# Ten of 24 gate tiles as five pairs of seven block products, in a stage of their own ahead of the attention

## The chip, the cores and the metric

The kernel runs on one NeuronCore of one Trainium2 chip. The metric is device time in microseconds of one execution of the whole program; lower is better. Several runs of one kernel are told by their median.

## The reference

One layer of a decoder trunk on 1024 tokens of width 1024, in float32:

```python
u = rmsnorm(x)
pool_v, q, k, v, f, z, xbc, dt, gate_logits = split_columns(u @ w_in)
y_A, y_B, y_C = pool(pool_v) @ p_pool, attention(q, k, v, f) @ p_attn, ssd(z, xbc, dt) @ p_ssd
g = sigmoid(gate_logits)                       # three gates of width 1024
x = x + (g[0] * y_A + g[1] * y_B + g[2] * y_C) @ w_out
x = x + conv_ffn(rmsnorm(x)) @ w_down          # conv_ffn: u @ w_up, causal conv, silu gate
```

The change concerns `gate_logits`: 3072 columns of the first product, handled as 24 tiles of 128 columns each.

## The kernel before, in words

Every product is a float32 product made of three products of a faster format: each operand is split into a high and a low part (`hi` by a copy on ScalarE, `lo` by a subtraction on VectorE), and `mm3` (L117) issues hi·hi, hi·lo and lo·hi into one PSUM bank. The normalized input stands transposed in SBUF for the whole first half, as `uh` and `ul`, two halves of 512 tokens each. One output tile (128 columns by 1024 tokens) takes 8 blocks of the inner dimension x 2 halves x 3 = 48 matmuls of 512 columns. `load_w` (L107) brings its weights (512 KB, one staging buffer `wraw`) and splits them into one of three buffer pairs `whi`, `wlo`.

Gate tile i is made by `gate` (L270): the product, a copy or sigmoid on ScalarE (L280, L282), and a store to `g_d` in DRAM, from where `gate_now` (L595) fetches it when a branch is merged. Tiles below `NGATE1` (L441) get their sigmoid at once, the others in `gate_now` (L602).

The stages in order:

1. Small projections, the pool mixer, then the SSD for two groups of heads (L581 to L584). The SSD's chunks are chains of small steps over all engines.
2. Eight gates (`run(gates())`, L585), with `p_big` as PSUM tile, then the values of the attention, `in_proj_tok` (L587), token by token: 8 tiles of 24 matmuls.
3. The attention, for four pairs of heads (L762 to L771). `attend` (L733) runs eight units per pair: scores (L673, L674), softmax on VectorE and ScalarE (L675 to L685), transposes of the probabilities (L697), their split (L702, L105), and the product with V (L722). `others` (L751) makes the queries and keys of the next pair (96 matmuls) and then the 5, 5, 4 and 2 gates that `GCUT` (L442) gives to each pair.
4. The merging of three branches (L784, L815, L818), the output product, and the feed-forward part. There the up product is already made in pairs of tiles by a scheme of seven block products in place of eight (`pair`, L1050, `prod`, L1007, `split_next`, L987): 2 x 2 blocks of weights and of the normalized input are added and subtracted beforehand, and their products combined after. Nine of the pairs have two products made earlier.

Each engine runs its instructions in an order that the framework fixes when the program is built, from a timeline of its own: what stands earlier in the program goes first, and where its operands are not ready in that timeline, later work is put in its place. So in the SSD and in the attention, gate products stand between the steps of the chains. The order does not change while the kernel runs.

Of the kernel before, what the change touches and what calls it, by code (L numbers as in the profile page):

```python
# [15 lines left out]
P = 128  # L16
# [30 lines left out]
def hybrid_kernel(ctx: ExitStack, tc: tile.TileContext, x, xT, w_in, w_z, w_v, w_fd, mixw, p_pool, p_attn,  # L47
# [33 lines left out]
    def bank():  # L81
        return pst("bank")
# [21 lines left out]
    def sub_lo(eng, lo, src, hi):  # L104
        eng.tensor_tensor(lo, src, hi.bitcast(F32), op=ALU.subtract)  # L105
# [93 lines left out]
    def run(gen):  # L199
        while True:  # L200
            try:
                next(gen)
            except StopIteration as e:
                return e.value
# [62 lines left out]

    g_d = dpool.tile([24, P, 1024], F32, name="g_d")

    def gate(i, halves):  # L270

        if halves:
            parts = in_proj_halves(T_GATE + i)
        else:
            ps = in_proj(T_GATE + i)
            parts = [(slice(h * 512, (h + 1) * 512), ps[:, h * 512:(h + 1) * 512]) for h in range(2)]
        for hs, ps in parts:
            gt = gpool.tile([P, 512], F32, name="gt")
            if i < NGATE1:
                nc.scalar.activation(gt, ps, AF.Sigmoid)  # L280
            else:
                nc.scalar.copy(gt, ps)  # L282
            nc.sync.dma_start(g_d[i][:, hs], gt)
# [157 lines left out]
    NGATE1 = 8  # L441
    GCUT = (0, 5, 10, 14, 16)  # L442
    v_d = dpool.tile([NATT, P, NT, 256], F32, name="v_d")
    yn_d = dpool.tile([NT, P, 1024], F32, name="yn_d")
    with ExitStack() as st:
# [130 lines left out]
        def gates():  # L576
            for i in range(NGATE1):
                gate(i, False)
                yield

# [4 lines left out]
        run(gates())  # L585

        for t, ps in in_proj_tok([w_v[kp, 0] for kp in range(4)], sp):  # L587
            vs = sp.tile([P, 8, 2, 64], R32, name="vs", tag="xs", bufs=5)
            pv = ps.rearrange("p (h d) -> p h d", d=64)
            nc.scalar.copy(vs[:, :, 0, :], pv)  # L590
            sub_lo(nc.vector, vs[:, :, 1, :], pv, vs[:, :, 0, :])
            nc.sync.dma_start(v_d[:, :, t, :].rearrange("r p c -> p r c"),
                              vs.bitcast(F32).rearrange("p (r h) x d -> p r (h x d)", h=2))
# [250 lines left out]
    def hl(t):  # L844
        return t[:, 0], t[:, 1]

    HL = [P, 2, 4, 512]
    LO, HI = slice(0, 512), slice(512, 1024)
    B11, B21, B22 = [hl(slot(i, HL, R32, n)) for i, n in enumerate(("b11", "b21", "b22"))]

    with ExitStack() as st:
# [77 lines left out]
        def up_load(n):  # L929

            if n < FT:
                q = 2 * ((n + 1) % 2)
                for x in range(2):
                    nc.sync.dma_start(ab[:, q + x, :], f_up[2 * ORDER[n] + x])

        for j in range(5):
            w = load_w(w_out[j])
            if j == 1:
                for i in range(2):
                    nc.sync.dma_start(ab[:, i, :], f_up[2 * i])  # L940
                up_load(0)
            for h in range(2):
                run(out_tile(j, h, w))
# [12 lines left out]

# [3 lines left out]
        LATE, ALL = ("S1", "S2", "S4", "S3"), ("A11", "S1", "S2", "A12", "S4", "S3")  # L960
        ring, parts = [], {}
        todo = []
        for n in range(FT + 1):
            names = [(n, name) for name in (() if n == FT else LATE if ORDER[n] < NPRE else ALL)]
            if n > 0:
                names.insert(names.index((n, "S2")) if names else 0, (n - 1, "A22"))
            todo += names
        n_split = [0]
        s12, s34 = None, ss

        def up_block(n, name):
            if name[0] == "S":
                t, c = (s12, s34)[(int(name[1]) - 1) // 2], (LO, HI)[(int(name[1]) - 1) % 2]
                return t[:, c]
            return ab[:, 2 * ((n + 1) % 2) + int(name[1]) - 1, (LO, HI)[int(name[2]) - 1]]

        SUMS = {"S1": ("A21", "A22", ALU.add), "S2": ("S1", "A11", ALU.subtract), "S3": ("A11", "A21", ALU.subtract),
                "S4": ("A12", "S2", ALU.subtract)}

        def up_sum(n, *names):  # L980

            if n < FT:
                for name in names:
                    x, y, op = SUMS[name]
                    nc.vector.tensor_tensor(up_block(n, name), up_block(n, x), up_block(n, y), op=op)

        def split_next():  # L987

            if n_split[0] == len(todo):
                return  # L990
            n, name = todo[n_split[0]]
            hi, lo = ring[n_split[0] % len(ring)]
            n_split[0] += 1
            src = up_block(n, name)
            nc.scalar.copy(hi, src)
            sub_lo(nc.vector, lo, src, hi)
            parts[n, name] = hi, lo
            if name == "A22":
                up_load(n + 2)
            if name == "S2":  # L1000
                if n == 0:
                    up_load(1)
                up_sum(n + 1, "S1", "S2")
            if name == "S3":
                up_sum(n + 1, "S4", "S3")

        def prod(ps, n, name, b, first=True):  # L1007

            w = parts[n, name]
            for k in range(4):  # L1010
                c = slice(k * P, (k + 1) * P)
                m = mm3([ps], (w[0][:, c], w[1][:, c]), [(b[0][:, k, :], b[1][:, k, :])], first and k == 0, k == 3,
                        skip_group_check=not first)
            split_next()
            return m

        def conv_act(i, ca, cb):

            v, g = [sp.tile([P, 1024], F32, name="vg", bufs=2) for _ in range(2)]
            for t, c, acc in ((2 * i + 1, cb, v), (2 * i, ca, g)):  # L1020
                w = [vec[:, V_FW + 3 * t + k:V_FW + 3 * t + k + 1] for k in range(3)]
                nc.scalar.activation(acc, c, AF.Identity, bias=vec[:, V_FB + t:V_FB + t + 1], scale=w[2])  # L1022
                for s in (1, 2):
                    nc.vector.scalar_tensor_tensor(out=acc[:, s:], in0=c[:, 0:1024 - s], scalar=w[2 - s],  # L1024
                                                   in1=acc[:, s:], op0=ALU.mult, op1=ALU.add)
            nc.scalar.activation(g, g, AF.Silu)
            nc.vector.tensor_tensor(g, g, v, op=ALU.mult)
            nc.sync.dma_start(act_d[i], g)
# [21 lines left out]
        def pair(n, c, last):  # L1050


            i = ORDER[n]
            ca, cb = c
            chain, b5 = bank(), bank()
            if i < NPRE:
                for x, t in ((0, cb[:, LO]), (1, ca[:, LO])):
                    nc.sync.dma_start(t, pre_d[i, x])
            else:
                prod(chain, n, "A11", B11)  # L1060
                nc.scalar.copy(ca[:, LO], chain)
            prod(b5, n, "S1", T1)
            nc.scalar.copy(cb[:, HI], b5)
            if last is not None:
                fourth(n - 1, *last)
            prod(chain, n, "S2", T2, first=i < NPRE)
            if i < NPRE:
                nc.tensor.matmul(chain, lhsT=ident, rhs=cb[:, LO], start=False, stop=True, skip_group_check=True)  # L1068
            nc.scalar.copy(ca[:, HI], chain)
            if i >= NPRE:  # L1070
                b2 = bank()
                prod(b2, n, "A12", B21)
                nc.vector.tensor_tensor(ca[:, LO], ca[:, LO], b2, op=ALU.add)
            prod(b5, n, "S4", B22, first=False)
            nc.vector.tensor_tensor(ca[:, HI], ca[:, HI], b5, op=ALU.add)
            prod(chain, n, "S3", T3, first=False)
            nc.vector.tensor_tensor(cb[:, HI], cb[:, HI], chain, op=ALU.add)
            return chain, c

        def fourth(n, chain, c):  # L1080
            prod(chain, n, "A22", T4, first=False)
            nc.scalar.copy(c[1][:, LO], chain)
            conv_act(ORDER[n], *c)

# [4 lines left out]
        for i in range(NPRE + 1):  # L1089
# [14 lines left out]
            if i == 2:  # L1104
                s12 = wpool.tile([P, 1024], F32, name="wraw", bufs=WRAW)
                up_sum(0, "S1", "S2", "S4", "S3")
# [4 lines left out]
        for _ in range(3):  # L1111
            hi, lo = [wpool.tile([P, 1024], R32, name=n, bufs=WHL) for n in ("whi", "wlo")]
            ring += [(hi[:, c], lo[:, c]) for c in (LO, HI)]
        ring += [(more[:, 0, r, :], more[:, 1, r, :]) for r in range(4)]
        for _ in range(len(ring)):
            split_next()
        last = None
        for i in range(FT):
            last = pair(i, (cc[:, 2 * (i % 2)], cc[:, 2 * (i % 2) + 1]), last)
        fourth(FT - 1, *last)  # L1120


# [205 lines left out]
```

## Time and profile before

| | before |
|---|---|
| time, median of 3 runs | 1877.31 us (1876.27 to 1879.17) |
| time of the profiled execution | 1876.14 us |
| its span, first to last instruction | 1874.4 us |
| TensorE busy | 98% of the span |
| VectorE busy | 58% |
| ScalarE busy | 46% |
| mean granted TensorE clock | 0.995 of full speed |

PE is TensorE, PEld its weight loads, DVE VectorE, ACT ScalarE, POOL GpSimd, SP the engine whose queue issues most transfers. Matmuls are pipelined: the recorded duration of one (about 0.39 us) overlaps the next, so what one costs is read as the distance between starts: the length of an unbroken piece divided by its matmuls. Some matmul records can be missing from a count.

### The profile page before, as it was taken

The page shows a single profiled execution, that of the slowest core. Times are in us where ns is not written, and L with a number is a line of the kernel's source. Part 1 is how long each engine was busy: PE and PEld are TensorE (multiplying, and loading weights), DVE is VectorE, ACT ScalarE, POOL GpSimd, SP SyncE. Part 2 cuts the span into 40 slices and gives each one's busy share as a digit, 9 for nine tenths or more (in the row PEclk, how much of TensorE's full clock was granted, in tenths as well). Part 3 has the DMA queues.
Part 4 walks back from the last instruction along what each step waited for, and adds up shares of the span by engine and source line. Part 5 has one row for each costly group of instructions (what it writes and reads, how often), then busy time and mean ns, then how long its engine had stood idle before and what let it go on. Part 6 is the DMA issues. An engine that isn't in the chain of part 4 may idle for free.

```text
span 1874.4 us, 22365 instructions
## 1 busy us (share of the span) xinstructions
PE 1841.7 (98%) x8622; PEld 1504.7 (80%) x8622; DVE 1086.6 (58%) x1611; ACT 856.8 (46%) x1384; POOL 157.1 (8%) x119
## 2 busy tenths in 40 slices
PE   7999999999999999999999999999999999999997
PEld 6888888888878778787788888878888888888886
DVE  6752682661265553655765432878787887743424
ACT  5343584573255463654633322545454555533221
POOL 0100240330000000000022002320000000000000
PEclk9999999999999999999999999999999999999998
DMA  4231231333511313124364451443333321664532
GB/s 153 84 120 34 85 108 57 101 130 104 175 65 62 107 51 129 40 90 153 121 200 135 145 180 68 152 135 124 102 107 118 104 91 53 214 235 157 180 102 68
DMA packets 81629, 217.35 MB, mean 116 GB/s; under 512 B 8625, under 2 KB 15217, under 8 KB 80754
## 3 DMA queue, kind: packets, MB, share of 16 engines
q1 hardware_dynamic: 76192, 201.82, 31.9%
q0 software_dynamic: 1728, 8.39, 1.4%
q10 hardware_dynamic: 3602, 5.72, 0.9%
q8 instruction: 67, 1.10, 0.2%
q14 instruction: 40, 0.33, 0.1%
HBM read 164.41 MB, written 51.48 MB: 115 GB/s over the span
## 4 chain that ended last, share of the span: by engine, by line
PE 93%; DVE 2%; DMA 2%; ACT 1%; issue 1%; POOL 0%; SPq 0%; DVEq 0%; ACTq 0%; POOLq 0%
PE p_bank L123 40%; PE p_big L123 19%; PE p_half L123 17%; PE p_bank L265 2%; PE p_bank L264 2%; PE p_bank L263 2%; PE p_po L722 2%; PE p_sc L674 2%; PE p_pt L697 2%; PE p_bank L557 1%; PE p_sc L673 1%; PE p_bank L1068 0%; DMA yi<-yn_d 0%; PE p_bank L324 0%; DMA ab<-in_f_up_dram 0%
## 5 line engine op out<-in xcount | busy, mean ns | idle before, releaser
L105 DVE TENSOR_TENSOR wlo<-wraw,whi 128x1024 fp32r<-128x1024 f32 (+1 forms) x109 | 126.3, 1159 | 162.8 <-ACT whi L112 161.3
L123 PE MATMUL p_bank<-act,whi 128*128 128x512 f32 (+1 forms) x736 | 218.5, 381 | 0.0
L123 PE MATMUL p_big<-uh,whi 128*128 128x512 f32 (+1 forms) x416 | 157.4, 379 | 0.5 <-ACT whi L112 0.5
L123 PE MATMUL p_big<-uh,wlo 128*128 128x512 f32 (+1 forms) x416 | 157.2, 378 | 0.5 <-DVE wlo L105 0.5
L123 PEld LDWEIGHTS p_bank<-act,whi 128*128 128x128 f32 x736 | 136.0, 188 | 26.6
L123 PE MATMUL p_big<-ul,whi 128*128 128x512 f32 (+1 forms) x416 | 156.7, 377 | 0.0
L123 PE MATMUL p_half<-uh,whi 128*128 128x512 f32 x384 | 153.4, 399 | 0.0
L123 PE MATMUL p_half<-ul,whi 128*128 128x512 f32 x384 | 153.0, 399 | 0.0
L123 PE MATMUL p_half<-uh,wlo 128*128 128x512 f32 x384 | 152.2, 397 | 0.0
L112 ACT CAST whi<-wraw 128x1024 fp32r<-128x1024 f32 x81 | 84.9, 1048 | 137.6 <-PE p_big L123 68.4
L123 PE MATMUL p_bank<-act,wlo 128*128 128x512 f32 (+1 forms) x368 | 139.2, 381 | 0.0
L123 PE MATMUL p_bank<-t,whi 128*128 128x512 f32 x440 | 137.2, 391 | 0.0
L123 PE MATMUL p_bank<-b,whi 128*128 128x512 f32 x376 | 118.9, 397 | 2.2 <-ACT whi L1046 2.0
L1024 DVE SCALAR_TENSOR_TENSOR vg<-cc,vec,vg 128x1023 f32<-128x1023 f32 (+1 forms) x88 | 110.3, 1278 | 8.4 <-ACT vg L1022 8.3
L105 DVE TENSOR_TENSOR wlo<-stage,whi 128x1024 fp32r<-128x1024 f32 x44 | 54.1, 1230 | 101.2 <-ACT whi L112 101.0
L112 ACT CAST whi<-stage 128x1024 fp32r<-128x1024 f32 x44 | 46.1, 1051 | 115.2 <-PE p_bank L123 106.7
L123 PEld LDWEIGHTS p_bank<-t,whi 128*128 128x128 f32 x440 | 82.6, 188 | 17.8
L123 PE MATMUL p_bank<-t,ring 128*128 128x512 f32 x396 | 96.4, 391 | 0.0
L172 POOL TENSOR_TENSOR ss<-ss,vg 128x512 f32<-128x512 f32 (+1 forms) x21 | 30.0, 1429 | 763.7 <-ACT vg L171 763.5
L123 PEld LDWEIGHTS p_big<-uh,wlo 128*128 128x128 f32 x416 | 78.9, 190 | 14.6 <-DVE wlo L105 0.8
L123 PEld LDWEIGHTS p_big<-uh,whi 128*128 128x128 f32 x416 | 79.0, 190 | 14.2 <-ACT whi L112 0.9
L123 PEld LDWEIGHTS p_big<-ul,whi 128*128 128x128 f32 x416 | 79.0, 190 | 13.5
(307 smaller groups left out, 4067.7 us busy)
## 6 DMA issues: line engine op xcount, KB each, us to landing
ab<-in_f_up_dram SPq DMA_DIRECT2D x53, 512.0 KB, 3.3
wraw<-in_w_in_dram SPq DMA_DIRECT2D x48, 512.0 KB, 3.4
stage<-in_f_down_dram SPq DMA_DIRECT2D x44, 512.0 KB, 3.5
g_d<-gt SPq DMA_DIRECT2D x48, 256.0 KB, 2.0
gt<-g_d SPq DMA_DIRECT2D x48, 256.0 KB, 3.4
act_d<-vg SPq DMA_DIRECT2D x22, 512.0 KB, 3.0
stage<-act_d SPq DMA_DIRECT2D x22, 512.0 KB, 4.5
mt<-acs_d SPq DMA_DIRECT2D x16, 512.0 KB, 4.4
```

Of the source, the lines that this page charges most:

```text
L105: eng.tensor_tensor(lo, src, hi.bitcast(F32), op=ALU.subtract)
L112: nc.scalar.copy(hi, raw)
L123: m = nc.tensor.matmul(o, lhsT=wt, rhs=ah[part], start=first and i == 0, stop=last and i == 2, **kw)
L172: eng.tensor_tensor(ss, ss, sq, op=ALU.add)
L263: nc.tensor.matmul(ps, lhsT=a, rhs=hi[:, c], start=k == 0, stop=False)
L264: nc.tensor.matmul(ps, lhsT=a, rhs=lo[:, c], start=False, stop=False)
L265: nc.tensor.matmul(ps, lhsT=ul[t // 4][:, k, q], rhs=hi[:, c], start=False, stop=k == NT - 1)
L557: nc.tensor.matmul(py[:, d], lhsT=mt[:, h * P:(h + 1) * P], rhs=xd[:, d], start=True, stop=True)
L674: nc.tensor.matmul(pss[:, 0:w], lhsT=Q2[h][hp, qs], rhs=KL[hp, j0:j0 + w], start=False, stop=True)
L697: nc.tensor.transpose(pt[:, off + (i - qq[0]) * P:off + (i - qq[0] + 1) * P], in_=probs[i][:, kb * P:(kb + 1) * P], identity=ident)
L722: nc.tensor.matmul(po[:, q0:q0 + w], lhsT=VV[:, kb, h, :], rhs=t[:, o:o + w], start=pc == 0 and i == 0, stop=last and i == len(prods) - 1)
L1024: nc.vector.scalar_tensor_tensor(out=acc[:, s:], in0=c[:, 0:1024 - s], scalar=w[2 - s], in1=acc[:, s:], op0=ALU.mult, op1=ALU.add)
```

## The change

The scheme of seven products becomes a class used in two places. The 24 gates are now made so: tiles 0 to 5 plainly beside the SSD; tiles 6 to 15 as five pairs in a new stage between the SSD and the attention; tiles 16 to 23 in the attention, 1, 2, 2 and 3 for its four pairs of heads. A pair splits seven 512-column blocks (A11, A12, A22 and four sums S1 to S4 of weight blocks), multiplies each with one block of the input (B11, B21, B22, or T1 to T4, which are sums of input blocks made once on VectorE while the values of the attention are multiplied), and combines the results on ScalarE and VectorE. Buffers: two pairs of raw weights `ab`, the three `whi`/`wlo` pairs as a ring of six half tiles, `s12` in the place of `wraw`, eight PSUM banks. `NGATE1` is 16, so 16 sigmoids in `gate_now` fall away and those 16 are taken when the gate is made. The feed-forward part uses the same class, with the calls in the order they had.

```diff
+    class BlockProduct:
+        LATE, ALL = ("S1", "S2", "S4", "S3"), ("A11", "S1", "S2", "A12", "S4", "S3")
+        SUMS = {"S1": ("A21", "A22", ALU.add), "S2": ("S1", "A11", ALU.subtract),
+                "S3": ("A11", "A21", ALU.subtract), "S4": ("A12", "S2", ALU.subtract)}
...
+        def load(self, n):
+            if n < len(self.order):
+                for x in range(2):
+                    nc.sync.dma_start(self.ab[:, 2 * ((n + 1) % 2) + x, :], self.src(self.order[n], x))
...
+        def split_next(self):
...
+            nc.scalar.copy(hi, src)
+            sub_lo(nc.vector, lo, src, hi)
+            self.parts[n, name] = hi, lo
+            if name == "A22":
+                self.load(n + 2)
+            if name == "S2":
+                if n == 0:
+                    self.load(1)
+                self.sums(n + 1, "S1", "S2")
+            if name == "S3":
+                self.sums(n + 1, "S4", "S3")
...
+        def prod(self, ps, n, name, b, first=True):
+            w, b = self.parts[n, name], self.blocks[b]
+            for k in range(4):
+                c = slice(k * P, (k + 1) * P)
+                mm3([ps], (w[0][:, c], w[1][:, c]), [(b[0][:, k, :], b[1][:, k, :])], first and k == 0, k == 3,
+                    skip_group_check=not first)
+            self.split_next()
...
-    NGATE1 = 8
-    GCUT = (0, 5, 10, 14, 16)
+    NPLAIN, NGATE1 = 6, 16
+    GCUT = (0, 1, 3, 5, 8)
...
-        run(gates())
-
-        for t, ps in in_proj_tok([w_v[kp, 0] for kp in range(4)], sp):
...
+        for i in range(NPLAIN):
+            gate(i, False)
+    psum(bank=(512, 8))
+    with ExitStack() as st:
+        tp = pool("t", stack=st)
...
+        def t_sums(sp):
+            for k in range(4):
+                f = {}
+                for n, h, k0 in (("T1", 0, k), ("T3", 1, k), ("T2", 1, k + 4), ("T4", 0, k + 4)):
+                    f[n] = sp.tile([P, 512], F32, name=f"f{n}", bufs=1)
+                    nc.vector.tensor_tensor(f[n], uh[h][:, k0, :].bitcast(F32), ul[h][:, k0, :].bitcast(F32),
+                                            op=ALU.add)
+                for n, x, y in (("T1", "T3", "T1"), ("T3", "T2", "T3"), ("T2", "T2", "T1"), ("T4", "T4", "T2")):
+                    nc.vector.tensor_tensor(f[n], f[x], f[y], op=ALU.subtract)
+                    hi, lo = blocks[n]
+                    nc.scalar.copy(hi[:, k, :], f[n])
+                    sub_lo(nc.vector, lo[:, k, :], f[n], hi[:, k, :])
+                yield
+        def gates_done(i, ca, cb):
+            for x, c in enumerate((ca, cb)):
+                for hs in (LO, HI):
+                    gt = gpool.tile([P, 512], F32, name="gt")
+                    nc.scalar.activation(gt, c[:, hs], AF.Sigmoid)
+                    nc.sync.dma_start(g_d[2 * i + x][:, hs], gt)
...
+        gp.load(0)
+        with ExitStack() as st2:
+            sp = pool("v", bufs=2, stack=st2)
+            ts = t_sums(sp)
+            for t, ps in in_proj_tok([w_v[kp, 0] for kp in range(4)], sp):
+                vs = sp.tile([P, 8, 2, 64], R32, name="vs", bufs=1)
...
+                next(ts, None)
+        gp.s12 = wpool.tile([P, 1024], F32, name="wraw", bufs=WRAW)
+        gp.sums(0, "S1", "S2", "S4", "S3")
+        sp = pool("gp", stack=st)
+        gp.run(w_ring(), sp.tile([P, 4, 1024], F32, name="cc"))
```

## Rows read from the trace of the kernel before

**Rows 1.** The page: span, busy time by engine, chain by engine.

```profile
span 1874.4 us, 22365 instructions
...
PE 1841.7 (98%) x8622; PEld 1504.7 (80%) x8622; DVE 1086.6 (58%) x1611; ACT 856.8 (46%) x1384; POOL 157.1 (8%) x119
...
PE 93%; DVE 2%; DMA 2%; ACT 1%; issue 1%; POOL 0%; SPq 0%; DVEq 0%; ACTq 0%; POOLq 0%
```

**Rows 2.** Busy time in stretches: SSD, gates and V, three head pairs, attention's end.

```profile
core 0: us, PE busy (x) PEld busy (x) DVE busy (x) ACT busy (x) POOL busy (x), PEclk, DMA share, GB/s
339.00:421.00 82.00, 80.89 (x440) 68.59 (x438) 58.16 (x85) 56.66 (x117) 32.85 (x24) 1.00 0.37 126
421.00:501.00 80.00, 80.00 (x357) 66.29 (x356) 14.84 (x22) 19.37 (x27) 1.30 (x1) 1.00 0.33 110
522.90:634.70 111.80, 111.80 (x537) 87.83 (x537) 60.46 (x118) 59.50 (x111) 0.53 (x1) 1.00 0.22 72
634.70:749.00 114.30, 114.30 (x543) 88.78 (x541) 60.62 (x118) 58.95 (x107) 0.53 (x1) 1.00 0.27 89
749.00:849.00 100.00, 100.00 (x484) 78.14 (x483) 57.09 (x113) 54.82 (x101) 0.00 (x0) 1.00 0.19 64
885.00:910.00 25.00, 20.94 (x107) 16.03 (x106) 18.92 (x42) 17.79 (x37) 0.00 (x0) 0.93 0.49 169
```

**Rows 3.** Chain in order of time: plain gates, gates in the attention, feed-forward pairs.

```profile
421.47 36.35 PE p_big L123 x160
...
523.76 5.71 PE p_half L123 x24
...
737.55 9.29 PE p_half L123 x41
...
1534.80 77.32 PE p_bank L123 x338
```

**Rows 4.** Groups by line in the first head pair, 522.9 to 634.7 us.

```profile
L123 PE MATMUL p_half<-uh,wlo 128*128 128x512 f32 x113 | 44.6, 395 | 0.0
...
L105 DVE TENSOR_TENSOR wlo<-wraw,whi 128x1024 fp32r<-128x1024 f32 x7 | 8.6, 1224 | 9.1 <-ACT whi L112 9.1
L112 ACT CAST whi<-wraw 128x1024 fp32r<-128x1024 f32 x8 | 8.4, 1047 | 9.0 <-PE p_half L123 6.3 <-DMA wraw<-in_w_in_dram 1.4 <-issue 1.3
L282 ACT COPY gt<-p_half 128x512 f32<-128x512 f32 x9 | 5.3, 585 | 6.3 <-PE p_half L123 6.3
```

**Rows 5.** Timeline of PE and DVE at two places of the first head pair.

```profile
565.09 0.71 PE L697 MATMUL p_pt<-cst,ns 128*128 128x128 f32 x5
...
566.30 0.69 DVE L105 TENSOR_TENSOR pl<-p_pt,ph 128x512 fp32r<-128x512 f32 x1 [0.20 <-ACT ph L702]
...
571.51 0.28 PE L722 MATMUL p_po<-pl,VV 128*128 128x256 f32 x1
...
582.28 0.60 PE L697 MATMUL p_pt<-cst,ns 128*128 128x128 f32 x4
...
583.53 0.69 DVE L105 TENSOR_TENSOR pl<-p_pt,ph 128x512 fp32r<-128x512 f32 x1 [0.24 <-ACT ph L702]
...
588.64 0.28 PE L722 MATMUL p_po<-pl,VV 128*128 128x256 f32 x1
```

**Rows 6.** Groups by line, 339 to 501 us: prices of 512-column steps.

```profile
L280 ACT ACTIVATE gt<-p_big 128x512 f32<-128x512 f32 x16 | 8.7, 595 | 0.1
...
L561 DVE TENSOR_TENSOR zs<-yt,zs 128x512 f32<-128x512 f32 x8 | 5.5, 684 | 0.1
...
L551 ACT CAST sth<-state 128x512 fp32r<-128x512 f32 x7 | 4.3, 615 | 0.0
```

**Rows 7.** Waits of DVE in the feed-forward pairs: total, times, longest.

```profile
DVE wraw L985 <- DMA ab<-in_f_up_dram: 24.8, 9, 4.5
```

More of the change, by code (lines that the diff above doesn't have):

```diff
@@ L268, in hybrid_kernel, with w_ring @@
+    def w_ring():
+        ring = []
+        for _ in range(WHL):
+            hi, lo = [wpool.tile([P, 1024], R32, name=n, bufs=WHL) for n in ("whi", "wlo")]
+            ring += [(hi[:, c], lo[:, c]) for c in (LO, HI)]
+        return ring
     g_d = dpool.tile([24, P, 1024], F32, name="g_d")
@@ L275, in gate @@
             ps = in_proj(T_GATE + i)
-            parts = [(slice(h * 512, (h + 1) * 512), ps[:, h * 512:(h + 1) * 512]) for h in range(2)]
+            parts = [(hs, ps[:, hs]) for hs in (LO, HI)]
         for hs, ps in parts:
@@ L574, in ssd_chunks @@
                 yield
[L576 to L579, printed above, removed]
         a0 = run(ssd_inputs(0))
@@ L584, in hybrid_kernel @@
         run(ssd_chunks(1, *a1))
-        run(gates())
-        for t, ps in in_proj_tok([w_v[kp, 0] for kp in range(4)], sp):
[L588 to L593, printed above, removed]
+        for i in range(NPLAIN):
+            gate(i, False)
@@ L842, in hybrid_kernel @@
     pre_d = dpool.tile([NPRE, 2, P, 512], F32, name="pre_d")
[L844 to L848, printed above, removed]
     B11, B21, B22 = [hl(slot(i, HL, R32, n)) for i, n in enumerate(("b11", "b21", "b22"))]
@@ L927, in hybrid_kernel, with conv_act, early_results @@
         ab = slot(3, [P, 4, 1024], F32, "ab")
[L929 to L934, printed above, removed]
+        def conv_act(i, ca, cb):
+            v, g = [sp.tile([P, 1024], F32, name="vg", bufs=2) for _ in range(2)]
+            for t, c, acc in ((2 * i + 1, cb, v), (2 * i, ca, g)):
+                w = [vec[:, V_FW + 3 * t + k:V_FW + 3 * t + k + 1] for k in range(3)]
+                nc.scalar.activation(acc, c, AF.Identity, bias=vec[:, V_FB + t:V_FB + t + 1], scale=w[2])
+                for s in (1, 2):
+                    nc.vector.scalar_tensor_tensor(out=acc[:, s:], in0=c[:, 0:1024 - s], scalar=w[2 - s],
+                                                   in1=acc[:, s:], op0=ALU.mult, op1=ALU.add)
+            nc.scalar.activation(g, g, AF.Silu)
+            nc.vector.tensor_tensor(g, g, v, op=ALU.mult)
+            nc.sync.dma_start(act_d[i], g)
+        def early_results(i, p1, c11):
+            for x, t in ((0, p1), (1, c11)):
+                nc.sync.dma_start(t, pre_d[i, x])
+        up_blocks = {"B11": B11, "B21": B21, "B22": B22}
+        up = BlockProduct(ORDER, lambda i, x: f_up[2 * i + x], up_blocks, ab, conv_act, NPRE, early_results)
+        up.s34 = ss
         for j in range(5):
@@ L940, in hybrid_kernel @@
                     nc.sync.dma_start(ab[:, i, :], f_up[2 * i])
-                up_load(0)
+                up.load(0)
             for h in range(2):
@@ L958, in hybrid_kernel @@
         T3, T4 = [hl(slot(4 + i, HL, R32, f"t{3 + i}")) for i in range(2)]
[L960 to L1028, printed above, removed]
+        up_blocks.update(T1=T1, T2=T2, T3=T3, T4=T4)
@@ L1048, in early_w @@
             return hi, lo
[L1050 to L1083, printed above, removed]
         ew = [early_w(i) for i in range(2)]
@@ L1104, in hybrid_kernel @@
             if i == 2:
-                s12 = wpool.tile([P, 1024], F32, name="wraw", bufs=WRAW)
-                up_sum(0, "S1", "S2", "S4", "S3")
+                up.s12 = wpool.tile([P, 1024], F32, name="wraw", bufs=WRAW)
+                up.sums(0, "S1", "S2", "S4", "S3")
         for _ in n:
@@ L1110, in hybrid_kernel @@
         cc = upool.tile([P, 4, 1024], F32, name="cc", tag="ul1")
[L1111 to L1120, printed above, removed]
+        up.run(w_ring() + [(more[:, 0, r, :], more[:, 1, r, :]) for r in range(4)], cc)
         stage = slot(3, [P, 4, 1024], F32, "stage")
```

79 lines of the change are left out of this document (added).

## The prediction

> **What bounds the kernel now.** I read the page first. TensorE is busy for 98% of the span, VectorE for 58%, ScalarE for 46%, and 93% of the chain that ended last is TensorE [rows 1]. A busy share can hide waits, because recorded durations overlap, so I went on to the stretches that the change touches. In each of them TensorE has work almost all the time: the second half of the SSD, the stretch with the remaining gates and V, and the attention, at a granted clock of 1.00, which is the 2.4 GHz level. Only at the end of the attention do 4.1 us in 25 stand idle, at a clock of 0.93 [rows 2]. The third view is the chain in order of time, for the distance between matmuls: 36.35 us for 160 plain gate matmuls, that is 0.2272 us each; 77.32 us for 338 in the feed-forward pairs, 0.2288 us; in the attention 0.2266 us (41 in a piece) to 0.2379 us (24 in a piece, the start of a piece after other work costs about 0.1 us more) [rows 3]. So every stretch is a queue of matmuls, and a matmul that goes is worth its distance, as long as those that stay still cover the waits of the SSD's and the attention's chains. That condition is the question of this change.
>
> **What goes and comes on TensorE.** Plain gates: two fewer before the attention, 2 x 48 = 96 matmuls x 0.2272 = 21.8 us less. They come out of the dense tail: 160 matmuls, 3.3 gates, run after the SSD has ended [rows 3], so with six gates 1.3 remain there and the SSD keeps all the cover it has. Gates in the attention: eight fewer, 384 matmuls; I take 0.232 us, between the two ends, so 89.1 us less (87.0 to 91.4). Five pairs of seven products of 12 matmuls: 420 matmuls at the distance of the same code in the feed-forward part, 0.2288 us, 96.1 us more [rows 3]. Sum: 96.1 - 21.8 - 89.1 = **-14.8 us** (-12.5 to -17.1). By count it is 60 matmuls of 512 columns fewer; the rest is that dense matmuls stand closer than scattered ones.
>
> The measured distance of 0.2272 us decides what 60 matmuls are worth [rows 3]. The Trainium skill, "TensorE: Matmul & The Clock Gate", section "Back-to-back issue gap", gives a sustained spacing of about 131 ns for 512 columns in a stream of loads and matmuls. By that the 60 would be worth 7.9 us and not 13.6; the trace does not agree, in any stretch that I read, so I keep the rows.
>
> **What is added beside it.** The sums for T1 to T4 are 12 VectorE steps of 512 columns for each of four k, 48 x 0.684 = 32.8 us, and 16 ScalarE casts x 0.615 = 9.8 us [rows 6]. They lie beside the last plain gates and the values of the attention: 80 us less 21.8 = 58.2 us of TensorE work, in which VectorE is busy for 14.84 us today [rows 2]. Two gates' splits go (2 x 1.22, [rows 4]), and four block sums (2.7) and the first six splits of the ring (4.1) come: 14.84 - 2.4 + 32.8 + 2.7 + 4.1 = 52.0 of 58.2 us. It fits, with little to spare; the first product that needs a T comes 12 matmuls, 2.7 us, after the values. Ends: 0 if it fits, 33 us if nothing were hidden. I take 1 us, since the row is near the first end, and 6 for the range, for the case that these steps start only when the plain gates are done.
>
> In a pair, VectorE has 7 splits, 4 sums and 3 additions, 14 x 0.684 = 9.6 us, and ScalarE 7 casts x 0.615, 4 copies and 4 sigmoids x 0.595 = 9.1 us [rows 6], against 19.2 us of matmuls: covered. The sums of a pair wait for its weights at the head of VectorE's queue, with the splits for the pair before it behind them; in the feed-forward part such a wait lasts at most 4.5 us [rows 7], and 338 matmuls run through it in one piece [rows 3]. The ring has six halves here, so five products, 13.7 us, lie between a split's start and its use: cost 0; without that cover it would be up to 4.5 us for each pair but the first, 18 us in all, and I leave it out of the range because the row shows it hidden. The stores of the gates are as many as before; ScalarE waits for one of two `gt` buffers in a pair, on no path.
>
> The new stage closes and opens the PSUM pools once more, drains the last pair, and the ring takes over the buffers of V's weights. The trace has no such place. Nearest: the change from V to the attention, inside the stretch to 501 us, without idle time, and the end of the attention with 4.1 us idle [rows 2]. I take 1 us, ends 0 and 4. The transfers are the same: ten weight tiles of 512 KB, loaded for a pair instead of one by one, on SP's queue, and V's loads for each head pair stay on POOL's in their old order. The 16 sigmoids that leave the merging are ScalarE's there and on no path: 0. The feed-forward part issues the same work: 0.
>
> **The attention with less to put between.** The first head pair takes 111.8 us [rows 2]. It holds 336 matmuls of queries, keys and gates (three groups, one of them shown [rows 4]), x 0.232 = 78 us, so the attention itself has 34 us of TensorE. VectorE is busy for 60.5 us and ScalarE for 59.5 [rows 2]. With one gate in place of five, TensorE has 34 + 22.3 + 11.1 = 67 us, VectorE 60.5 - 4 x 1.22 = 55.6, ScalarE 59.5 - 4 x 1.05 - 8 x 0.585 = 50.6 [rows 4]. The second and third pairs get two gates: 78 us of TensorE against 57 on VectorE at most. The fourth has no queries to make, but three gates, 67 us, and then the merging's products. So TensorE remains the longest everywhere, by 11 to 21 us.
>
> Do the waits inside the chains fit? At 565.1 us five transposes start; their split `pl` is finished at 566.99, and the product that needs it is issued at 571.51: about 5.9 us of other work lie there, of which 1.4 were needed. At 582.3 the transposes end at 582.6, `pl` at 584.22, the product starts at 588.64: 1.6 of 6.0 us [rows 5]. So a quarter of the work put between is needed as cover, and half of it stays (156 us of 245). Cost: 0 if the new order spreads what is left and lets the next head pair's scores begin while one ends; 89 us if nothing could move up. I take 2 us, near the low end, because of the quarter.
>
> **Sum:** -14.8 + 1 + 1 + 2 = -10.8 us. The profiled execution took 1876.14 us (its span plus 1.7); 1865.3. The median of the runs lies 1.2 us above it: **1866.5 us**.
>
> **Rivals.**
> *Uncovered chains in the attention (slower).* The order puts other work wherever the chain is not ready, so what is left may be used up early in each head pair, and then the chain runs alone. Missing are 4, 3 and 2 gates in the first three pairs, 9 x 11.1 = 100 us, a quarter of which was needed [rows 5]: 25 us of waiting. Then -14.8 + 25 + 2 = +12 us, 1889.5 us. It decides from 13 us of waiting on. For it: VectorE's 55.6 us come near TensorE's 67 in the first pair, and the softmax is a chain over three engines. Against it: the margin of three quarters. Where TensorE stands idle the clock may follow, as 0.93 shows [rows 2]; at half rate for a seventh of those 25 us it cost under 2 us.
> *The gain is given back piece by piece.* T sums late (6), the stage's ends (4), the attention (4): -0.8 us, about 1876.5 us. For it: 52 of 58 us on VectorE leaves little. Against it: three costs would all have to be near their upper ends.
>
> That the change does not do what it says I can exclude for the counts: they follow from the loops.
>
> **How the numbers follow.** Forecast 0.74, uncovered chains 0.14, given back 0.12. About 0.2% (3.8 us) is what a measurement of this kernel can tell from no change, so faster 0.74, same 0.12, slower 0.14. The range begins at 1858: -17.1 with no added cost gives 1860.2, and 2 us of the idle time at the attention's end [rows 2] might go too. It ends at 1880: the forecast with T sums 5, the ends 3 and the attention 5 us dearer is 1879.5, which takes in the piecewise rival. Outside lie most of the uncovered chains and a little below, under 0.2 together.
>
> **What would show it.** Right: 420 matmuls in about 96 us between V and the attention, without idle time; the stretch from the SSD's end to V's end about 58 us; the attention shorter by 85 us or more, its TensorE without waits for `pl` or the softmax. Wrong: PE waiting for VectorE's `lo` of a T or a ring half at the first pair; PE waiting for `ns` or `pl` late in each head pair, 13 us and more in sum; the clock below 0.97 in the attention.

## The result, and the profile after

The changed kernel takes 1892.06 us (median of 4 runs, 1891.63 to 1893.5) against 1877.82 us in 4 runs of the kernel before beside it: a ratio of 1.0077, with a 95% interval of 1.006 to 1.0095. It is **slower**, by 14 us. The profiled execution took 1892.17 us.

The page of the changed kernel (span, busy time, chain by engine):

```profile
span 1890.4 us, 22429 instructions
...
PE 1842.6 (97%) x8562; PEld 1504.7 (80%) x8562; DVE 1146.4 (61%) x1719; ACT 878.2 (46%) x1429; POOL 155.9 (8%) x119
...
PE 93%; DVE 3%; DMA 2%; ACT 1%; issue 1%; POOL 0%; SPq 0%; DVEq 0%; ACTq 0%; POOLq 0%
```

Beside [rows 1], TensorE has the 60 matmuls fewer, and VectorE 60 us more work. TensorE's share fell by one point, so the page alone doesn't tell where the time went. The starts of four products in the two traces cut the span into stretches:

| stretch | before | after | difference | by the prediction |
|---|---|---|---|---|
| start to the first query product of the attention | 501.2 | 581.1 | +79.9 | 96.1 - 21.8 = +74.3 |
| from there to the first product of the second branch (`oh`) | 455.8 | 383.6 | -72.2 | -89.1 |
| from there to the first product of the third branch (`yn`) | 50.0 | 57.3 | +7.3 | 0 |
| from there to the last matmul | 860.6 | 861.7 | +1.1 | 0 |
| sum | | | +16.0 | -14.8 |

So 30.8 us are missing: 5.6 in the new stage, 16.9 in the attention, 7.3 at the start of the second branch, 1.1 in the rest. Busy time by stretch after the change (values, pairs, first head pair, second, third, the end of the attention, second branch):

```profile
core 0: us, PE busy (x) PEld busy (x) DVE busy (x) ACT busy (x) POOL busy (x), PEclk, DMA share, GB/s
...
436.00:485.00 49.00, 45.60 (x194) 37.47 (x194) 34.04 (x56) 18.78 (x31) 0.00 (x0) 0.97 0.28 97
485.00:581.10 96.10, 95.32 (x421) 78.60 (x421) 43.53 (x65) 41.04 (x69) 0.00 (x0) 1.00 0.31 103
602.80:677.00 74.20, 73.69 (x346) 55.60 (x346) 47.36 (x85) 43.62 (x73) 0.00 (x0) 1.00 0.13 43
677.00:760.00 83.00, 79.71 (x397) 61.45 (x395) 54.53 (x113) 50.34 (x96) 0.53 (x1) 1.00 0.22 70
760.00:842.00 82.00, 79.81 (x372) 61.45 (x372) 46.69 (x95) 45.44 (x87) 0.53 (x1) 0.98 0.24 78
...
868.80:910.00 41.20, 34.86 (x140) 24.76 (x140) 30.93 (x63) 25.65 (x48) 2.12 (x4) 0.79 0.47 156
...
964.60:1022.00 57.40, 53.50 (x257) 44.02 (x257) 40.39 (x52) 12.44 (x21) 18.98 (x15) 0.97 0.63 197
```

The pairs take the forecast 96.1 us with TensorE busy throughout. The first head pair is tight too; the second and third have 3.3 and 2.2 us idle, and the end of the attention 6.3 of 41.2 us at a clock of 0.79, where [rows 2] had 4.1 of 25 at 0.93. The whole attention, up to the second branch, before and then after:

```profile
501.20:957.00 455.80, 451.74 (x2162) 354.50 (x2160) 257.18 (x496) 236.10 (x434) 6.55 (x12) 1.00 0.31 103
```

```profile
581.10:964.60 383.50, 370.90 (x1761) 286.98 (x1759) 238.29 (x480) 214.22 (x405) 6.56 (x12) 0.97 0.29 94
```

TensorE is idle for 12.6 us in place of 4.1. So 8.5 of the missing 16.9 us are idle time; the rest is in work that takes longer, at a mean clock of 0.97 in place of 1.00, which over 383.5 us is worth up to about 11 us (an estimate, since the clock also counts while TensorE is idle). What TensorE waited for, from the end of the SSD to the third branch:

```profile
PE p_sc L839 <- DVE ns L841: 6.4, 5, 2.2
PE p_bank L977 <- DVE yi L973: 3.8, 2, 3.1
PE p_half L123 <- DMA yps<-yp_d: 3.5, 1, 3.5
PE p_bank L263 <- ACT gt L405: 3.4, 1, 3.4
PE p_po L888 <- DVE pl L105: 2.4, 2, 2.2
```

L839 and L840 are the scores, L841 the first step of the softmax, L888 the product with V. The first row is new, and 6.0 of its 6.4 us lie in the first three head pairs: TensorE stands ahead of a score product because the score banks are still being read. The chain in order of time shows the places:

```profile
437.11 1.28 ACT L405
438.40 1.09 ACT gt L405 x2
484.98 92.49 PE p_bank L123 x408
...
751.64 1.27 DVE ns L841 x2
...
758.13 1.07 DVE pl L105 x2
...
869.32 8.33 DMA yps<-yp_d
...
966.43 6.09 DMA yi<-yn_d
```

At 437 us the pool change waits for the last plain gate's sigmoids, a table load of 1.28 us ahead of them. At 752 and 758 us the softmax and the split of the probabilities stand on the path, with no gate left in that head pair. `yps` lies in the space of `uh` and `ul`, which the last gate reads until 869.0 us; until it lands there is only the attention's chain to run. And the first load of `yi`, which lies in space that the attention held, starts behind the last product with V: 1.1 us behind 938.57 before, 2.4 us behind 963.99 after. That product was 18.4 us ahead of the second branch; now it is 0.7 us ahead, and the load is in the open. The first load stands in these rows of the tile `yi`, before and then after (duration min/median/max, first and last start):

```profile
L806 SPq DMA_DIRECT2D yi<-yn_d x16: 319/376/1342, 939.7 to 989.7; - x16
```

```profile
L972 SPq DMA_DIRECT2D yi<-yn_d x16: 319/370/730, 966.4 to 1015.8; - x16
```

The clock shows in the score products of 512 columns. The timeline of PE in the changed kernel, at two places:

```profile
689.01 0.40 PE L839 MATMUL p_sc<-K,Q 128*128 128x512 f32 x1
689.34 0.49 PE L840 MATMUL p_sc<-KL,Q 64*128 64x512 f32 x1
```

```profile
897.25 0.79 PE L839 MATMUL p_sc<-K,Q 128*128 128x512 f32 x1
897.97 0.79 PE L840 MATMUL p_sc<-KL,Q 64*128 64x512 f32 x1
```

The distance within the pair is 0.33 us in the first place and 0.72 us in the second, 28 us into the stretch with clock 0.79 and behind most of its idle time; from 897 to 910 us the granted clock is 0.56. So the end of the attention runs in part at 1.2 GHz, and that makes its chain longer still.

### The profile page after: what moved, and what is told of

Same layout as the page of the kernel before. It is cut to its first block, busy times and chain, and to the rows that moved or that the text cites. A ratio compares the mean times of both kernels' runs of the same rounds, so it can differ in the third digit from the quotient of the medians.

```text
span 1890.4 us, 22429 instructions
## 1 busy us (share of the span) xinstructions
PE 1842.6 (97%) x8562; PEld 1504.7 (80%) x8562; DVE 1146.4 (61%) x1719; ACT 878.2 (46%) x1429; POOL 155.9 (8%) x119
## 4 chain that ended last, share of the span: by engine, by line
PE 93%; DVE 3%; DMA 2%; ACT 1%; issue 1%; POOL 0%; SPq 0%; DVEq 0%; ACTq 0%; POOLq 0%
PE p_bank L123 45%; PE p_big L123 18%; PE p_half L123 12%; PE p_bank L263 2%; PE p_bank L265 2%; PE p_bank L264 2%; PE p_po L888 2%; PE p_sc L840 2%; PE p_pt L863 1%; PE p_bank L683 1%; PE p_sc L839 1%; DMA yi<-yn_d 1%; DMA yps<-yp_d 0%; PE p_bank L359 0%; PE p_bank L977 0%
## 5 line engine op out<-in xcount | busy, mean ns | idle before, releaser
L123 PE MATMUL p_big<-uh,whi 128*128 128x512 f32 (+1 forms) x384 | 145.5, 379 | 1.3 <-ACT whi L112 1.3
L123 PE MATMUL p_big<-uh,wlo 128*128 128x512 f32 (+1 forms) x384 | 145.3, 379 | 0.5 <-DVE wlo L105 0.5
L123 PE MATMUL p_big<-ul,whi 128*128 128x512 f32 (+1 forms) x384 | 144.8, 377 | 0.0
L112 ACT CAST whi<-wraw 128x1024 fp32r<-128x1024 f32 x71 | 74.4, 1049 | 114.0 <-PE p_big L123 62.6
L123 PE MATMUL p_half<-uh,whi 128*128 128x512 f32 x256 | 103.3, 404 | 0.0
L123 PE MATMUL p_half<-uh,wlo 128*128 128x512 f32 x256 | 102.2, 399 | 0.0
L123 PE MATMUL p_half<-ul,whi 128*128 128x512 f32 x256 | 102.1, 399 | 0.0
L841 DVE SCALAR_TENSOR_TENSOR ns<-crow,cum,p_sc 128x512 f32<-128x512 f32 (+2 forms) x96 | 55.9, 608 | 56.7 <-PE p_pt L863 44.3
L123 PEld LDWEIGHTS p_bank<-t,ring 128*128 128x128 f32 x396 | 74.3, 188 | 16.3
L123 PEld LDWEIGHTS p_bank<-b,whi 128*128 128x128 f32 x376 | 71.0, 190 | 19.8 <-ACT whi L1152 2.5
```

Source lines behind the costliest of these rows:

```text
L112: nc.scalar.copy(hi, raw)
L123: m = nc.tensor.matmul(o, lhsT=wt, rhs=ah[part], start=first and i == 0, stop=last and i == 2, **kw)
L841: nc.vector.scalar_tensor_tensor(out=ns[:, j0:j0 + w], in0=crow[:, j0:j0 + w], scalar=cum[:, qi, hd:hd + 1], in1=pss[:, 0:w], op0=ALU.subt ...
```

## The experiments

Unless the text says otherwise, the edit is made in the changed kernel. All were timed against the kernel before (medians of 1877.26 to 1877.51 us).

**Where the loss is: in the pairs or in the attention.**

e1, the kernel before with only the places of the gates changed:

```diff
-    NGATE1 = 8
-    GCUT = (0, 5, 10, 14, 16)
+    NGATE1 = 16
+    GCUT = (0, 1, 3, 5, 8)
```

> The kernel before with sixteen plain gates ahead of the attention and eight in it (1, 2, 2, 3 by head pair): no block products, no new stage, the same number of matmuls as before. Theory A (the attention's own chains end its stage once its gates are gone): eight tiles cost 8 x 48 x 0.2272 = 87 us ahead, the attention gives back 55 to 65 of 89 us, so 22 to 32 us over before, 1900 to 1910 us. Theory B (the new stage with seven products is what costs): nothing of it is here, so 1875 to 1880 us. Theory C (the loss sits in the last head pair and the merging behind it, by the way the gates are spread): as A in sum, but with no waits in the first three head pairs.

Measured: 1899.46 us, ratio 1.0108 (1.0093 to 1.0123), just under theory A's range: the attention gave back 70 us and not 55 to 65. Nothing is new in this kernel, no pair, no stage, no sum, and by matmuls it should have stood still. The attention takes 385.7 us and the second branch 57.2, as in the changed kernel, and all 4.4 us of waits for `ns` lie in the first three head pairs, which theory C excludes. The loss comes from moving gates out of the attention.

e2, one pair ahead, the gates of the attention as before:

```diff
-    NPLAIN, NGATE1 = 6, 16
-    GCUT = (0, 1, 3, 5, 8)
+    NPLAIN, NGATE1 = 6, 8
+    GCUT = (0, 5, 10, 14, 16)
```

> The changed kernel with only one pair in the new stage (six plain gates, one pair, sixteen gates in the attention as before: 5, 5, 4, 2). T sums, PSUM change and ring are all there; the products save 12 matmuls, 2.7 us. Theory A and C: the stage costs what its two visible waits cost (3.8 us at the PSUM change, 1.2 us at the pair), so 1.5 to 4 us over before, 1879 to 1882 us. Theory B: the stage costs most of the 29 us that are missing, so 1890 us or more.

Measured: 1882.43 us, ratio 1.0028 (1.0018 to 1.0038), just above the range of theories A and C and far from B's. From the attention's first product to the second branch 455.7 us, as before (455.8): with sixteen gates nothing is lost there. The attention starts at 505.35, 4.2 us later, where the matmuls alone say 2.6 us earlier (19.2 - 21.8): the stage costs 6.8 us with one pair, where it cost 5.6 with five.

e4, the eight gates put later:

```diff
-    GCUT = (0, 1, 3, 5, 8)
+    GCUT = (0, 0, 1, 3, 8)
```

> The changed kernel, its eight attention gates spread 0, 1, 2, 5 over the head pairs in place of 1, 2, 2, 3. Theory C (loss in the last head pair and behind it): the last pair has 55 us to put between in place of 33, so 5 to 9 us less, 1883 to 1887 us. Theory A (too little cover as a whole): what the last pair gains the first ones lose, 1889 to 1896 us. Theory B: no difference, 1892 us.

Measured: 1898.03 us, ratio 1.0102 (1.0082 to 1.0122), on theory A's side and 2 us above its range. The second branch is back at 50.7 us, but the attention takes 394.7: the waits of scores for `ns` are as long (6.1 us) and those for `pl` doubled (4.7 us). What one head pair gets, another lacks: this other cut of the same sum doesn't help.

e5, no gate in the attention, nine pairs ahead of it:

```diff
-    NPLAIN, NGATE1 = 6, 16
-    GCUT = (0, 1, 3, 5, 8)
+    NPLAIN, NGATE1 = 6, 24
+    GCUT = (0, 0, 0, 0, 0)
```

> The changed kernel with no gate left in the attention: the eight are made ahead, as four more pairs of seven products (76.8 us more there by 19.2 a pair, 85.4 fewer matmul time in the attention by 384 x 0.2224). Theory A (the attention has a floor set by its chains, and the first eight gates taken out already reached it in part): the stretch from the attention's first query product to the second branch's first product falls by 40 us or less, from 383.5 to 343 or more, and the total is 1925 or more. If all of the 85 us came off, the total would be about 1884.

Measured: 1916.12 us, ratio 1.0209 (1.0194 to 1.0224): between the two numbers. The attention's stretch fell by 54.9 us to 328.7, so the floor is not as hard as theory A had it, and the other 30 of the 85 us are lost. That stretch, and 14 us near its end:

```profile
657.70:986.40 328.70, 303.96 (x1374) 229.42 (x1372) 226.90 (x470) 197.29 (x379) 6.55 (x12) 0.90 0.25 84
908.00:922.00 14.00, 5.93 (x23) 4.59 (x22) 8.10 (x16) 10.58 (x17) 0.00 (x0) 0.50 0.38 132
```

TensorE is idle for 24.7 us, VectorE and ScalarE are far from full, and in the 14 us, of which TensorE is idle for 8.1, the granted clock is 0.50, the 1.2 GHz level.

**Whether it is the chain.** The same step of the softmax is left out of both kernels, in every head: the division of the probabilities by their sum. It makes the chain from score to product shorter and leaves TensorE's work as it is; VectorE and ScalarE have a step less for each row of scores:

```diff
-            rs = sp.tile([P, 1], F32, name="rs", bufs=4)
-            nc.vector.reciprocal(rs, sm)
-            nc.scalar.activation(ns[:, 0:n], ns[:, 0:n], AF.Copy, scale=rs)
```

> The changed kernel with the division by the softmax sum left out in every head (one reciprocal on VectorE and one copy on ScalarE fewer between the exponential and the transposes), so its output is not the attention's. Theory A (with eight gates in place of sixteen TensorE runs out of other work in the attention, and waits for the chain score, softmax, transpose, product): the chain is about a fifth shorter, the waits of head pairs two and three and of the last pair (about 16 us in sum) shrink, and the attention's start to its last product falls by 8 us or more; total 1876 to 1885. Theory B (TensorE is not waiting for the chain; the matmuls are only spaced more widely, or the transfers at the end decide): no more than 3 us less, 1889 to 1893. Its twin on the kernel before tells what the missing step is worth where there is cover.

> The kernel before with the same step of the softmax left out (the division by the sum, in every head). Theory A: with sixteen gates the chain was covered, so the time stays within 3 us of 1877. Theory B (ScalarE or the chain already bounded the attention before): 8 us less or more, as in the changed kernel.

Measured: the changed kernel 1885.19 us (1879.92 to 1886.13), 6.9 us less; the kernel before 1882.44 us, 5.1 us more. With a short chain the change costs 2.7 us, with the whole chain 14.2. In the changed kernel's trace, which is of the fastest of its four runs, the time from the attention's first product to its last product with V fell from 382.9 to 361.7 us, up to the second branch only from 383.6 to 378.1, the second branch from 57.3 to 51.6. The waits for `ns` fell from 6.4 to 1.5 us, those for `pl` did not (2.6 after 2.4), and the clock of the stretch from 868 to 910 us is 0.92:

```profile
868.00:910.00 42.00, 37.85 (x178) 28.34 (x177) 30.76 (x57) 22.33 (x45) 2.31 (x5) 0.92 0.57 192
```

That a shorter chain helps the changed kernel and not the one before is what theory A says, though the first time lies at the edge of its range and the second 2 us outside. The 5.1 us more in the kernel before, no theory had: a softmax of another length gets another order from the framework, and kernels that differ in the order alone are some us apart (below); that this is the cause here was not tried. So the sizes are good to about 5 us. The opposite signs agree with the chain as the cause; that it is the length of the chain and not the work of VectorE or ScalarE as such, this pair of runs does not part.

**What the stage costs.** e3, the change of PSUM pools put behind the values:

```diff
-    psum(bank=(512, 8))
     with ExitStack() as st:
...
+        psum(bank=(512, 8))
         gp.s12 = wpool.tile([P, 1024], F32, name="wraw", bufs=WRAW)
```

> The changed kernel, with the change to eight PSUM banks moved from before the attention's values to behind them. All theories: if the 3.8 us wait at 436 us comes from the PSUM change alone, it goes and nothing takes its place: 3 to 4 us under the changed kernel, 1888 to 1889 us. If V's start waits for something else, or the pairs' start inherits the wait, 1891 to 1893 us.

Measured: 1896.03 us, ratio 1.008 (1.0057 to 1.0104), a miss. The wait ahead of the values went, another of about its size came ahead of the first product with a T, and the attention starts 0.4 us earlier only. (Its order came out another, and it takes 390.4 us: with the same gates in the same places.) The waits of PE and of ACT in its stage, 425 to 510 us:

```profile
PE p_bank L123 <- ACT cc L352: 3.6, 1, 3.6
```

```profile
ACT vs L750 <- DMA v_d<-vs: 14.0, 5, 3.7
ACT cc L352 <- DMA v_d<-vs: 3.3, 1, 3.3
```

e10 took it for VectorE being late with the T sums, and gave 16 of their additions to GpSimd besides:

```diff
-                    nc.vector.tensor_tensor(f[n], uh[h][:, k0, :].bitcast(F32), ...
+                    nc.gpsimd.tensor_tensor(f[n], uh[h][:, k0, :].bitcast(F32), ...
```

> The changed kernel with the sixteen additions of the T sums on GpSimd in place of VectorE, and the change of the PSUM pools behind the values of the attention in place of ahead of them. If the two waits of the new stage (3.8 us for the last plain gate's sigmoids ahead of the values, 4.0 us for T in the run that only moved the pools) are each a wait for one engine, both go: attention's start at 576 to 578 in place of 581.1, total 1887 to 1889 if the attention's order stays. If GpSimd's additions slow VectorE or are slow themselves, the first product with a T waits 4 us or more and nothing is won: 1891 to 1896.

Measured: 1898.22 us, ratio 1.0117 (1.0102 to 1.0132): the attention starts 9.5 us later than in the changed kernel, the second of the two cases and 2 us above its range. TensorE waits 5.9 us for `cc`, behind the store of `vs` still, and 4.4 us for two of VectorE's splits of weights. The rows of the sums (ns, min/median/max) show why VectorE is late:

```profile
L725 DVE TENSOR_TENSOR fT<-fT,fT x16: 677/682/1778, 430.2 to 465.9; 128x512 f32<-128x512 f32 x16
...
L105 DVE TENSOR_TENSOR T<-fT,T x16: 675/680/1794, 431.6 to 467.7; 128x512 fp32r<-128x512 f32 x16
L722 POOL TENSOR_TENSOR fT<-uh,ul x12: 1292/1674/1737, 433.0 to 461.9; 128x512 f32<-128x512 f32 x12
```

An addition takes GpSimd 1.67 us where VectorE took 0.68, and some of VectorE's own now take up to 1.79, 1.1 us more than the others: most of one of GpSimd's additions, the shortest of which took 1.29. The Trainium skill, "SBUF — State Buffer", section "SBUF: two separate sides", says that the two engines lock a shared pair of ports for whole instructions; these maxima agree with that.

The rows of e3 above name the second cause: ScalarE stands 14.0 us behind the store of `vs`, of which the change keeps one buffer (five before), and the first pair's copy `cc` is queued behind it. e12 gives it a second buffer, in the space of two block sums that are free until then:

```diff
+            vs_ = (sp.tile([P, 8, 2, 64], R32, name="vs", bufs=1),
+                   gp.s34.bitcast(R32).rearrange("p (h x d) -> p h x d", x=2, d=64))
...
-                vs = sp.tile([P, 8, 2, 64], R32, name="vs", bufs=1)
+                vs = vs_[t % 2]
```

together with the pool change of e3.

> The changed kernel with the change of the PSUM pools behind the values and with two buffers for the split values (the second one is the space of the pair's third and fourth sum, free until then), where the changed kernel has one and ScalarE waits 13.0 us in it for the store. Theory D (the stage's second wait, 4.0 us ahead of the first product with a T in the run that only moved the pools, is ScalarE standing behind the store of the values, not VectorE being late with the T sums): both waits go, attention's start at 576 to 577.5 in place of 581.1. Theory E (the T sums themselves are too much for VectorE there): attention's start stays at 580 or later. Total by D 1887 to 1890 where the attention's order stays.

Measured: 1884.55 us, ratio 1.0044 (1.003 to 1.0057), theory D, and 2.5 us below its range. The attention starts at 574.93, 6.2 us earlier than in the changed kernel and where the matmuls alone put it (501.2 + 74.3 = 575.5); it takes 383.1 us and the second branch 57.3, unchanged. Neither edit is enough by itself as far as was tried: the later pool change alone gave 0.4 us (e3), and a second buffer with the pool change in its old place was not run. The stage with the values is full at full clock:

```profile
436.00:480.00 44.00, 44.00 (x195) 36.43 (x195) 32.05 (x51) 17.41 (x29) 0.00 (x0) 1.00 0.32 108
```

**How many gates may go.** e15: stage as in e12 but without any change of pools, sixteen gates in the attention, and two plain gates fewer beside the SSD:

```diff
-    NPLAIN, NGATE1 = 6, 16
-    GCUT = (0, 1, 3, 5, 8)
+    NPLAIN, NGATE1 = 4, 8
+    GCUT = (0, 5, 10, 14, 16)
```

> Sixteen gates stay in the attention (5, 5, 4 and 2, as before), four plain ones stand beside the SSD, and four are made as two pairs; no change of the PSUM pools for them (their products use the four banks that are there), and two buffers for the split values. Matmuls: four plain gates less, 192 x 0.2272 = 43.6 us, two pairs more, 38.4 us: 5.2 us less. Theory A (only the gates taken out of the attention cost cover; the SSD needs fewer than the 4.7 it used): attention as before (455 to 457 us), total 1871 to 1876, the first kernel here below the one before. Theory F (the SSD's end lacks the 0.7 gates, or the stage still costs what one pair showed, 6.8 us): 1878 to 1886.

Measured: 1882.93 us, ratio 1.0031 (1.002 to 1.0043), theory F. The attention is as before: it takes 458.3 us from its first query product, but that product stands 3.5 us earlier ahead of the first scores here, and from the first scores to the second branch it is 433.1 us against 434.0. TensorE waits for a new step, the state at the end of the SSD's chain (0.5 us in the kernel before and in the changed one):

```profile
PE p_bank L123 <- ACT sth L677: 6.2, 1, 6.2
```

From 400 to 436 us the granted clock is 0.81, where it is 1.00 in the changed kernel. The SSD needs more than four plain gates as cover; six, as in the change, were enough.

e17 and e18: twelve gates in the attention, three pairs ahead, six plain ones, the stage of e12; in e18 another cut and no change of pools.

```diff
-    NPLAIN, NGATE1 = 6, 16
-    GCUT = (0, 1, 3, 5, 8)
+    NPLAIN, NGATE1 = 6, 12
+    GCUT = (0, 3, 6, 9, 12)
```

> Twelve gates stay in the attention, three to a head pair, six plain ones beside the SSD, three pairs of products; pools and split values as in e12_v_two. Matmuls: two plain gates less (21.8 us), three pairs more (57.6), four gates fewer in the attention (192 x 0.2224 to 0.232 = 42.7 to 44.5): 6.9 to 8.7 less. Theory A with a threshold (twelve gates still cover the chains): 1868 to 1873. Theory A with a loss that grows with every gate taken out (18 us of 87 were lost for eight, so 9 for four, with the second branch's start): 1877 to 1882.

> As e17_twelve_left, but the cut of the twelve gates is 3, 2, 3 and 4 by head pair, and the PSUM pools aren't changed for the pairs. In e17_twelve_left the first three head pairs show no wait of over 0.7 us, and the last one and the start of the second branch show 8.4 us in six waits. If the last head pair lacked cover there, up to 4 us of these go, and the 0.3 us of the pool change: 1871 to 1874. If these waits are for the transfers of yps and the addition ahead of the second branch, whatever the cut, or the second head pair now lacks cover: 1875 to 1879.

Measured: e17 (cut 3, 3, 3, 3) 1875.19 us, ratio 0.9992 (0.9983 to 1.0001); e18 (cut 3, 2, 3, 4) 1876.76 us, ratio 0.9999 (0.999 to 1.0008). e17 lies between its two cases: its attention takes 415.4 us, 40.4 less for 42.7 to 44.5 us of matmuls, its second branch 51.0. Its longest waits from the SSD's end to the third branch:

```profile
PE p_big L123 <- DVE mg L789: 1.6, 1, 1.6
PE p_half L123 <- DMA yps<-yp_d: 1.6, 1, 1.6
PE p_bank L979 <- DVE yi L975: 1.2, 1, 1.2
PE p_sc L841 <- DVE ns L843: 0.8, 1, 0.8
```

No wait in this list is longer than 1.6 us. e18's gates for the last head pair brought nothing: its waits for `pl` are 3.8 us in sum (0.2 in e17), and those for `yps`, the addition (`mg`) and `yi` stay, the second of its two cases. e17 is 17 us faster than the changed kernel, but no version here is faster than the kernel before by more than the 0.2% that can be told.

## Why the prediction was wrong

**Right.** Two plain gates fewer and five pairs more: with the stage's waits removed, the attention starts at 574.93 against 575.5 forecast (e12), and the pairs take 96.1 us against 96.1. The distances of the rows held (0.2272 and 0.2288 us): 92.49 us for 408 matmuls are 0.2267. The T sums fit beside the values, as 52 of 58 us said: in e12 VectorE is busy for 32.05 of the 44 us.

**The step that failed** is the attention's cover: "So a quarter of the work put between is needed as cover, and half of it stays", and from it "I take 2 us, near the low end, because of the quarter". It cost 16.9 us in the attention and 7.3 in the second branch. The quarter was read at one step of the chain, the split `pl`, in the first head pair, which had five gates [rows 5]; that pair stayed tight even with one. The largest new wait came at another step, scores behind `ns`, in the second and third pairs, and the rest at the end, where nothing but the chain is left. Sums of busy time over a head pair said only that no engine is full ("TensorE remains the longest everywhere"), which is true even in e5; they don't say whether a chain over three engines is covered. Two slips of its sums weigh little: 156 of 245 us are 64% and not half, and the end of -12.5 us for TensorE should be -12.7.

The prices of one gate show it best, from the lengths of the attention and the second branch together:

| gates left in the attention | attention + second branch | gained for each gate taken out |
|---|---|---|
| 16 (before) | 455.8 + 50.0 = 505.8 | |
| 12 (e17) | 415.4 + 51.0 = 466.4 | 9.9 |
| 8 (the change) | 383.6 + 57.3 = 440.8 | 6.4 |
| 0 (e5) | 328.7 + 62.1 = 390.8 | 6.3 |

A gate in a pair costs 96.1 / 10 = 9.6 us. The first four taken out gain 9.9 and cost 9.6 each, so almost nothing is left; the next four gain 6.4 each and lose 12.8 us together. With the plain gates' gain (21.8 - 19.2 = 2.6), the stage's loss (5.6) and the 1.1 of the rest, that is -2.6 - 1.0 + 12.8 + 5.6 + 1.1 = +15.9 us, the span's +16.0. The prediction valued each at 11.1. Each row is one order of the framework: with the other traces of eight gates (440.3 us in e12, 437.0 to 446.4 in the others) the second step is 5.0 to 7.4 us for a gate, so the fall from 9.9 holds, its size less so.

**The terms that were too small.** "The new stage ... I take 1 us, ends 0 and 4", and 1 us for the T sums: 5.6 us measured, 6.2 taken away by e12. Two causes stand one behind the other. The pool change was weighed, too low: TensorE waits 3.4 us there. The one buffer of `vs`, which stands in the diff, was not costed at all, and shows as soon as the pool change is out of the way (3.6 us in e3). The second branch was at nothing, and the prediction does not name the loads of `yi`; what hid them before was the 18 us by which the attention's last product was ahead. The other runs agree: with 13 us or more ahead the second branch takes 50.0 to 53.4 us (before, e2, e4, e8, e9, e15, e17, e18), with less than 1 us 55.9 to 57.3 (the change, e1, e3, e10, e12). The feed-forward part, costed at 0, took 1.1 us more; why was not tried.

**The rival** "uncovered chains" had the place, the side and nearly the time, 1889.5 us against 1892.06, with 27 us against 30.8 missing; of it 24.2 are in the attention and the second branch, 5.6 in the stage, which it had as 2, and 1.1 in the rest. That its 25 us came so near is in part luck: they are a quarter of 100, the quarter read at the wrong step; 7.3 us of the loss lie in the second branch, which it did not have; and TensorE's waits for `ns` and `pl` are 8.8 us in sum, under the 13 that the prediction set as its sign. What the argument against it called the margin of three quarters was the failed step.

What stays open: how the 16.9 us divide between waiting and the slower clock beyond the estimate above, as no run parts the two; whether a fourth bank for the scores or a better order of the same work would save part of it, which no run tried; and what the order alone does. Kernels with the same eight gates in the same places have attentions of 380.6 us (e10), 383.1 (e12), 383.6 (the change), 385.7 (e1) and 390.4 (e3). TensorE is idle for 10.4 to 12.6 us in each; the shortest has the highest mean clock (0.98) and the longest the lowest (0.95).

## What to carry to other kernels

Work that stands between the steps of a chain has two prices, its own time and the cover that it gives; take some of it out in steps and compare what each step gains with what it costs elsewhere, since here the first four gates taken out were worth 9.9 us each and the next four 6.4. Before counting on cover, read the whole chain at its barest place (its end, its last unit), not one step where work is plenty, and see what is released by the chain's last instruction. In a diff, a buffer count that falls from five to one is a cost to be worked out like any instruction.

## What the runs showed of the hardware beside this

Additions on GpSimd beside VectorE made both slower (e10): 1.67 us in the median on GpSimd, the shortest 1.29, and up to 1.79 us on VectorE, the median 0.68. The clock's answer to idle time is local: 0.79 over the 41 us at the attention's end after the change, 0.92 there with the shorter chain (e8), and 0.50 over 14 us of e5 in which TensorE was busy for 5.9, with 1.00 in the stretches of the changed kernel that had work throughout.
